# Weight sums of seven-product matrix multiplications: on the engines, or by copying and adding transfers in DRAM

## The chip, the core and the metric

The kernel runs on one core of a Trainium2 chip. The metric is the device time of one execution in microseconds; three runs of the kernel before gave 787.34, 787.57 and 787.62 us, a median of 787.57. The engines are named as in the profile: PE multiplies matrices, PEld loads its weights, DVE, ACT and POOL work on tiles, SP only issues transfers. Transfers are issued from the queue of SP, ACT or POOL, and all of them run on the same 16 DMA engines.

## What is computed

One decoder block on 512 positions of width 1024, in float32:

```python
h = rmsnorm(x, norm1_g);  z = h @ w_in + b_in          # (512, 1024) @ (1024, 6656)
u = glu(z);  u = conv31(u);  u = silu(layernorm(u));  y_a = u @ conv_w_out + conv_b_out
xb = conv4(z_rx);  hb = rg_lru(xb);  y_b = (hb * gelu(z_rg)) @ lru_w_out
m = sigmoid(z_ga) * y_a + sigmoid(z_gb) * y_b;  x = x + m @ w_mix_out
h = rmsnorm(x, norm2_g)
x = x + (silu(h @ ffn_w1) * (h @ ffn_w3)) @ ffn_w2      # (512,1024)@(1024,2816), twice; (512,2816)@(2816,1024)
out = rmsnorm(x, norm_f_g)
```

## The kernel before

**Precision.** Every float32 matrix is split into a high part (a rounded copy, made on ACT) and a low part (what the rounding took away, made by a subtraction on DVE or POOL, line 119). A product is the sum of three: high by high, high by low, low by high. A weight chunk is 128 x 1024 numbers (512 KB): SP loads it into one of four `raw` buffers, ACT casts it into one of five `hl` slots (line 123), DVE or POOL makes the low part, PE uses it. `weights(key, ahead)` makes chunks ready up to four chunks ahead of the one in use.

**Stages.** First projection (`z`, 52 tiles of 24 products, about 23 to 310 us), with the depthwise convolution on DVE and the gates of the recurrence (the `h` entries, `g` in the profile) running beside it in the order that the string `ORDER` writes out; then `yb` (the recurrence's output product), `ya` (the convolution's), the mixing product (`mxr`), the SwiGLU products (`f` for the first pair of tiles, `fr` for the others) and the last product (`or`).

**Seven products for eight.** The mixing product, ten of the eleven pairs of SwiGLU tiles (`SEVEN`, k = 1 to 10) and the last product go by a scheme of seven half-size products in place of eight (Strassen's, in Winograd's form). For it, weights are taken in quarters b11, b12, b21, b22, and four sums of quarters are needed: t1 = b12 - b11, t3 = b22 - b12, t2 = t3 + b11, t4 = b21 - t2. The activations get sums of their own (`pair`, `f_inputs`). For the mixing product the sums are made on DVE (`make_sums`, line 321), before and after.

**The sums for SwiGLU and the last product, before.** They are made in pieces of 128 x 1024 numbers: load four quarters to a `wsum` buffer (`piece_load`, line 396), four operations in place (`piece_sums`, lines 119 and 407), store four sums to DRAM (`piece_store`, line 413). There are 40 pieces for SwiGLU and 22 for the last product. In the first projection, `yb` and `ya` a generator (`make_f_sums`) takes one step per entry of `ORDER`, per tile of `yb` and per tile of `ya`: its loads are on SP's queue, its sums on POOL, its stores first on SP's, later on POOL's queue. From the SwiGLU stage on `out_step` starts the pieces of the last product after the plan `OUT_PIECES`: load and store on POOL's queue, sums on DVE. `tc.issue_after(...)` places an instruction behind another one on its engine. In the z stage PE, ACT, DVE and SP follow the written order; POOL is ordered by the planner, behind those marks.

**Pairing.** A pair k of SwiGLU tiles is the neighbours 2k and 2k + 1, and so are the two tiles of the last product's k. Two neighbours lie side by side in DRAM, so chunks of 256 columns are loaded (`f_chunks`: rows of 1 KB for the quarters, and 4 KB without a break for the stored sums); only b11, and all chunks of k = 1, 2, 3 but t2 and t1, are loaded by `f_both` in rows of 128 columns.

Of the kernel before, what the change touches and what calls it, by code (L numbers as in the profile page):

```python
# [35 lines left out]
SUMS_BEHIND = 3  # L36
# [11 lines left out]
PIECES = 4  # L48


OUT_PIECES = {0: "1", 1: "111", 2: "01", 3: "11", 4: "111", 5: "101", 6: "111", 7: "111", 8: "101", 9: "101", 10: "100"}
# [4 lines left out]
SUMS_AT, SUMS_STEP, SUMS_LAG, STORE_LAG = 3, 3, 2, 2  # L56
STORED_LAG = 3
SUMS_DENSE, SUMS_OWN, SUMS_EACH = 22, 40, (56, 68)


F_LATE, F_AT, OUT_MIX, MIX_LATE_LAG, LATE_LAG = 2, 6, 1, 2, 8
OUT_IN = 0
# [23 lines left out]
def tile_block(ctx, tc, a, out):  # L86
# [5 lines left out]
    wsums = pool("wsums", PIECES)  # L92
# [20 lines left out]


# [150 lines left out]
    class Quartered:  # L265
        def __init__(self, name, w, kh, lo, parts=(), step=None, on_pool=(), put_off=()):
# [3 lines left out]
            self.step = step or 1  # L270
            self.tile = lambda k, i: k + kh * i if self.step == 1 else 2 * k + i
# [3 lines left out]
            self.sums = {(n, k): self.all_sums[k][:, i, :] for i, n in enumerate(IN_PLACE) if n not in parts for k in range(kh)}  # L275
# [45 lines left out]
        def make_sums(self, k):  # L321
# [8 lines left out]
            if not self.parts:  # L330
                for i, v in enumerate(q):
                    nc.sync.dma_start(self.all_sums[k][:, 2 * i : 2 * i + 2, :], v.rearrange("p (m n) -> p m n", m=2))
                return
# [20 lines left out]
    WHERE = {  # L354
        "b21": ("b2", 0, True), "b22": ("b2", 1, False), "t2": ("t0", 0, True),
        "t1": ("t0", 1, False), "t3": ("t1", 1, True), "t4": ("t1", 0, False),
    }

    def f_both(n, k, lo=vec):

        def load(raw_t):
            for i, w_ in enumerate((w1, w3)):
                if n[0] == "b":
                    src = f_quarter(n, k, w_, 0, 4)
                else:
                    c, e, _ = WHERE[n]
                    src = f_sums[k][:, i, int(c[1]), :].rearrange("p (k n) -> p k n", k=4)[:, :, e * P : (e + 1) * P]
                newest["any"] = nc.sync.dma_start(raw_t[:, i * T : (i + 1) * T].rearrange("p (k n) -> p k n", k=4), src).ins

        wchunk(f"f{n}_{k}", load, 8, P, lo=lo)  # L370

    def f_chunks(k, some=("b2", "t0", "t1")):

        for n in some:
            for i, w_ in enumerate((w1, w3)):
                if n == "b2":
                    src = w_[:, 4:8, 2 * k * P : 2 * (k + 1) * P]
                else:
                    src = f_sums[k][:, i, int(n[1]), :].rearrange("p (k n) -> p k n", k=4)
                wchunk(f"f{n}{i}_{k}", src, 4, 2 * P, lo=vec)  # L380

    def f_piece(k, i, c):

        quarters = (w1, w3)[i].rearrange("p (h n) c -> p n h c", n=2)[:, c, :, 2 * k * P : 2 * (k + 1) * P]
        return f"{k}_{i}_{c}", [quarters], f_sums[k][:, i].rearrange("p m (k c n) -> p c m k n", k=2, c=2)[:, c]

    def o_piece(k, c):
        four = outq.w.rearrange("p (k h) (e n) -> p h k e n", h=2, e=2)
        cs = slice(256 * c, 256 * c + 256)
        return f"o{k}_{c}", [four[:, h, k, :, cs] for h in range(2)], outq.all_sums[k][:, :, cs]  # L390

    def piece_load(name, halves, queue=nc.sync):
        raw = wsums.tile([P, 1024], F32, tag="wsum", name=f"fws{name}")
        n = 1024 // len(halves)
        for h, src in enumerate(halves):
            queue.dma_start(raw[:, h * n : h * n + n].rearrange("p (e n) -> p e n", n=256), src)  # L396
        return raw

    def piece_sums(raw, dest, eng):
        if len(dest.shape) == 4:  # L400
            of = raw.rearrange("p (h k e n) -> p h e k n", h=2, k=2, e=2)
        else:
            of = raw.rearrange("p (h e n) -> p h e n", h=2, e=2)
        q11, q12, q21, q22 = (of[:, h, e] for h in range(2) for e in range(2))
        sub(eng, q22, q22, q12)
        sub(eng, q12, q12, q11)
        eng.tensor_tensor(out=q11, in0=q22, in1=q11, op=ALU.add)
        sub(eng, q21, q21, q11)

    def piece_store(raw, dest, queue=nc.sync):  # L410
        if len(dest.shape) == 4:
            dest = dest.rearrange("p m k n -> p (m k) n")
        return queue.dma_start(dest, raw.rearrange("p (m n) -> p m n", n=256))  # L413

    def make_f_sums():

        todo = f_todo[:-F_LATE] + [out_todo.pop(0) for _ in range(OUT_IN)]
        sums_due, stores_due = [], []
        n, next_at, stored = 0, SUMS_AT, [-9]
        while todo or sums_due or stores_due:
            if stores_due and (emitted[0] >= stores_due[0][0] or not (todo or sums_due)):
                stores_due.pop(0)[1]()
                stored[0] = n
            if sums_due and n >= sums_due[0][0]:
                sums_due.pop(0)[1]()
            if todo and n >= next_at and len(sums_due) + len(stores_due) + (n < stored[0] + STORED_LAG) < PIECES:  # L430
                next_at += SUMS_STEP - (n >= SUMS_DENSE) - (SUMS_EACH[0] <= n < SUMS_EACH[1])
                name, halves, dest = todo.pop(0)
                with tc.issue_after(newest["load"]):
                    raw = piece_load(name, halves)

                def sums(raw=raw, dest=dest, own=n >= SUMS_OWN):
                    with tc.issue_after(newest["sub"]):
                        piece_sums(raw, dest, pool_e)
                        if own:
                            piece_store(raw, dest, pool_e)  # L440
                            return

                    def stores():
# [1283 lines left out]
```

## Time and profile before

| | |
|---|---|
| median of three runs | 787.57 us (787.34 to 787.62) |
| profiled execution: span | 785.7 us |
| PE busy | 777.9 us, 99% |
| DVE busy | 682.8 us, 87% |
| ACT busy | 474.6 us, 60% |
| POOL busy | 362.3 us, 46% |
| SP's queue: packets, MB, share of 16 engines | 178066, 161.80, 68.4% |
| POOL's queue (software): packets, MB, share | 10272, 36.18, 13.2% |
| granted clock of PE | 0.998 |

The profiled execution took 785.7 us from its first to its last instruction; the runs' 787.57 us has about 1.9 us beside that span. A group of instructions reads: line, engine, operation, output <- inputs, how often, then busy time, mean of one, and the idle time of the engine just before with what ended it. A row of the chain of waits reads: start, length, what. A row of a stage has the busy time of PE, PEld, DVE, ACT and POOL with their counts of instructions, the granted clock, the mean busy share of the 16 DMA engines and GB/s. A row of a DMA queue has packets, MB and the share of 16 engines' time; a row of transfers has the issuing queue, how many, their size and, on POOL's queue, the median time to landing.

### The profile page before, as it was taken

The numbers are of one execution on the slowest core, as the hardware profiler recorded it, in microseconds if no ns is written. First come the engines' busy times: TensorE is split into PE (matmuls) and PEld (weight loads), VectorE is DVE, ScalarE is ACT, GpSimd is POOL, SyncE is SP. The second block draws the span as 40 slices with busy tenths as digits, with TensorE's granted clock in tenths as the row PEclk, the third lists the DMA queues.
The fourth block names the chain that finished last, engine by engine and source line by source line (L and its number), as shares of the span: only waits on it lengthen the run. The fifth ranks groups of instructions, "written<-read, shape, count | busy, mean of one in ns | idle before, by whom it ended". The sixth has DMA issues, their size and how long they took to land.

```text
span 785.7 us, 12502 instructions
## 1 busy us (share of the span) xinstructions
PE 777.9 (99%) x4327; PEld 680.0 (87%) x4327; DVE 682.8 (87%) x1074; ACT 474.6 (60%) x697; POOL 362.3 (46%) x353
## 2 busy tenths in 40 slices
PE   9999999999999999999999999999999999999996
PEld 8888888888888888888888898999999999888885
DVE  6389998889987988999799869899878888999956
ACT  8543678966785786574235675555554555556844
POOL 4367876789798988654440382122322321000000
PEclk9999999999999999999999999999999999999999
DMA  8556989899899966998978676699998998778652
GB/s 246 164 148 183 290 227 271 239 275 275 249 278 272 274 203 208 331 303 268 306 264 294 189 211 209 192 313 313 348 339 297 325 333 283 226 237 273 196 172 108
DMA packets 188561, 199.04 MB, mean 253 GB/s; under 512 B 15290, under 2 KB 149586, under 8 KB 188498
## 3 DMA queue, kind: packets, MB, share of 16 engines
q1 hardware_dynamic: 178066, 161.80, 68.4%
q0 software_dynamic: 10272, 36.18, 13.2%
q8 instruction: 34, 0.56, 0.3%
q14 instruction: 29, 0.24, 0.1%
q10 hardware_dynamic: 160, 0.27, 0.1%
HBM read 146.30 MB, written 38.80 MB: 236 GB/s over the span
## 4 chain that ended last, share of the span: by engine, by line
PE 98%; DMA 1%; DVE 0%; ACT 0%; SPq 0%; issue 0%
PE z L577 36%; PE fr L1440 25%; PE or L1204 13%; PE yb L577 7%; PE ya L577 6%; PE mxr L1204 5%; PE f L577 3%; PE g L1030 2%; PE fr L1495 1%; DMA x<-in_x_dram 1%; PE tx L638 0%; PE th L622 0%; PE z L695 0%; ACT of L1668 0%; PE orl L1204 0%; DVE n1j L659 0%
## 5 line engine op out<-in xcount | busy, mean ns | idle before, releaser
L830 DVE SCALAR_TENSOR_TENSOR cv<-u,par,cv 128x507 f32<-128x507 f32 (+15 forms) x240 | 162.2, 733 | 4.2 <-ACT cv L826 3.3
L119 POOL TENSOR_TENSOR hl_in<-raw_in,hl_in 128x1024 fp32r<-128x1024 f32 (+1 forms) x52 | 123.8, 2391 | 53.8 <-ACT hl_in L123 44.7
L119 POOL TENSOR_TENSOR fws<-fws 128x256 f32<-128x256 f32 x114 | 92.0, 810 | 44.1 <-DMA fws<-in_ffn_w_dram 38.8
L413 POOL DMA_DIRECT2D ot<-fwso x21 | 15.4, 733 | 132.9 <-DVE fwso L119 125.0
L1440 PE MATMUL fr<-hs_0h,hl_ft 128*128 128x256 f32 x320 | 59.2, 283 | 0.0
L123 ACT CAST hl_ft<-raw_ft 128x1024 fp32r<-128x1024 f32 x40 | 41.7, 1046 | 27.2 <-PE fr L1440 18.5
L119 DVE TENSOR_TENSOR hl_ft<-raw_ft,hl_ft 128x1024 fp32r<-128x1024 f32 x39 | 47.7, 1222 | 10.9 <-ACT hl_ft L123 10.8
L123 ACT CAST hl_in<-raw_in 128x1024 fp32r<-128x1024 f32 x50 | 51.4, 1047 | 1.7 <-PE z L577 1.1
L1440 PEld LDWEIGHTS fr<-hs_0h,hl_ft 128*128 128x128 f32 x320 | 50.6, 192 | 0.0
L1440 PE MATMUL fr<-hs_0l,hl_ft 128*128 128x256 f32 x160 | 45.3, 283 | 0.0
L119 DVE TENSOR_TENSOR hl_fb<-raw_fb,hl_fb 128x1024 fp32r<-128x1024 f32 x29 | 35.5, 1225 | 9.3 <-ACT hl_fb L123 9.3
L123 ACT CAST hl_fb<-raw_fb 128x1024 fp32r<-128x1024 f32 x30 | 31.5, 1049 | 17.9 <-PE fr L1440 8.8
L577 PE MATMUL z<-h10h,hl_in 128*128 128x512 f32 (+1 forms) x108 | 41.1, 382 | 0.0
L577 PE MATMUL z<-h12h,hl_in 128*128 128x512 f32 (+1 forms) x108 | 40.8, 379 | 0.0
L577 PE MATMUL z<-h13h,hl_in 128*128 128x512 f32 (+1 forms) x108 | 40.8, 379 | 0.0
L577 PE MATMUL z<-h14h,hl_in 128*128 128x512 f32 (+1 forms) x108 | 40.8, 379 | 0.0
L577 PE MATMUL z<-h15h,hl_in 128*128 128x512 f32 (+1 forms) x108 | 40.8, 379 | 0.0
L577 PE MATMUL z<-h16h,hl_in 128*128 128x512 f32 (+1 forms) x108 | 40.8, 379 | 0.0
L577 PE MATMUL z<-h11h,hl_in 128*128 128x512 f32 (+1 forms) x108 | 40.8, 379 | 0.0
L577 PE MATMUL z<-h17h,hl_in 128*128 128x512 f32 (+1 forms) x108 | 40.8, 379 | 0.0
L396 POOL DMA_DIRECT2D fwso<-in_ffn_w_dram x42 | 29.9, 716 | 23.7 <-DMA ot<-fwso 21.9
L119 POOL TENSOR_TENSOR hl_ot<-raw_ot,hl_ot 128x1024 fp32r<-128x1024 f32 x1 | 2.4, 2413 | 83.2 <-ACT hl_ot L123 83.2
(949 smaller groups left out, 2629.6 us busy)
## 6 DMA issues: line engine op xcount, KB each, us to landing
raw_in<-in_w_in_dram SPq DMA_DIRECT2D x51, 512.0 KB
fws<-in_ffn_w_dram SPq DMA_DIRECT2D x38, 512.0 KB
raw_ft<-fs SPq DMA_DIRECT2D x34, 512.0 KB
fs<-fws POOLq DMA_DIRECT2D x25, 512.0 KB, 5.2
fwso<-in_ffn_w_dram POOLq DMA_DIRECT2D x42, 256.0 KB, 7.1
ot<-fwso POOLq DMA_DIRECT2D x21, 512.0 KB, 6.0
raw_ob<-in_ffn_w_dram SPq DMA_DIRECT2D x33, 256.0 KB
raw_ot<-ot SPq DMA_DIRECT2D x33, 256.0 KB
```

The source lines that it names most:

```text
L119: return eng.tensor_tensor(out=o, in0=x, in1=y, op=ALU.subtract)
L123: copy(h, full)
L396: queue.dma_start(raw[:, h * n : h * n + n].rearrange("p (e n) -> p e n", n=256), src)
L413: return queue.dma_start(dest, raw.rearrange("p (m n) -> p m n", n=256))
L577: pe.matmul(ps, l, r, start=i == 0, stop=i == n - 1)
L830: vec.scalar_tensor_tensor(out=acc[:, s:], in0=u[c][:, : T - s], scalar=dw(c, s), in1=acc[:, s:], op0=ALU.mult, op1=ALU.add)
L1030: pe.matmul(ps[:HB], head_chunk[0][:ROWS_G, g, h % 2, m, :], ext[h][m][:ROWS_G], start=m == 0, stop=m == 1)
L1204: pe.matmul(banks[i][:, cs], l_[:, ts], r_[:, cs], start=start and n == 0, stop=stop and n == 2, skip_group_check=again)
L1440: pe.matmul(ps[:, HALVES[i]], lw[:, c, :], rx_, start=not (again or i or c or m), stop=bool(i and c == 3 and m == 2), skip_group_check=True,)
L1495: pe.matmul(self.r4[:, HALVES[i]], lw, rx_, start=not (i or c or m), stop=bool(i and c == 3 and m == 2), skip_group_check=True)
```

## The change

The sums for SwiGLU and the last product are made without any engine: transfers from DRAM to DRAM copy a quarter into the place of a sum, and adding transfers (with an accumulating operation) add another quarter to what lies there. They are issued from POOL's queue. Since a transfer can add but not subtract, the scheme is written with plus signs in the weights (t3 = b12 + b22, t2 = t3 + b11, t4 = t2 + b21, t1 = b11 + b12), and the minus signs go to the sums of activations and of results: `add` becomes `sub` and the other way round in `pair`, `f_inputs`, `rest`, `mix_end` and `out_end`. `make_sums` for the mixing product gets plus signs too and stays on DVE.

Tiles are paired eleven apart (k and k + 11), so that a transfer for SwiGLU covers ten tiles at once: 128 rows of 1280 numbers (5120 bytes), one for each of four chunks of rows, two weights and eight steps of the sums: 64 transfers of 655 KB. Those of the last product cover up to three k: 128 x 3 rows of 2 KB: 24 of 786 KB and 8 of 524 KB. Each sum is a list in which every transfer needs the one before: six long (t3, t2, t4) or two long (t1). Four lists take turns. One transfer is issued per step of the generator; there is a step per entry of `ORDER` (60, the first three empty), 12 in `yb`, 8 in `ya` and two for each k in the SwiGLU loop.

The SwiGLU chunks are now all loaded by `f_both`: two transfers of 256 KB, in rows of 128 columns (512 bytes). The low parts of `lo` and `co` chunks are made on POOL instead of DVE, and so are those of b22 and t3 for k from 4 on.

```diff
-            wchunk(f"lo{j}_{hf}", lru_out[:, 5 * hf : 5 * hf + 5, j * P : (j + 1) * P], 5, P, lo=vec)
+            wchunk(f"lo{j}_{hf}", lru_out[:, 5 * hf : 5 * hf + 5, j * P : (j + 1) * P], 5, P)
...
-        wchunk(f"co{j}", conv_out[:, :, j * P : (j + 1) * P], ND, P, lo=vec)
+        wchunk(f"co{j}", conv_out[:, :, j * P : (j + 1) * P], ND, P)
...
-            self.all_sums = [dram.tile([P, 4, T], F32, tag=f"{name}t_{k}", name=f"{name}t_{k}") for k in range(kh)]
+            self.all_sums = {n: dram.tile([P, kh, T], F32, tag=f"{name}{n}", name=f"{name}{n}") for n in IN_PLACE if n not in parts}
...
-            sub(vec, q22, q22, q12)
-            sub(vec, q12, q12, q11)
-            vec.tensor_tensor(out=q11, in0=q22, in1=q11, op=ALU.add)
-            sub(vec, q21, q21, q11)
+            add(q22, q22, q12)
+            add(q12, q12, q11)
+            add(q11, q22, q11)
+            add(q21, q21, q11)
...
-    f_sums = {k: dram.tile([P, 2, 2, 1024], F32, tag=f"fs{k}", name=f"fs{k}") for k in SEVEN}
+    f_sums = {(n, i): dram.tile([P, 4, KF * P], F32, tag=f"fs{n}{i}", name=f"fs{n}{i}") for n in IN_PLACE for i in range(2)}
+    f_cols = slice(min(SEVEN) * P, KF * P)
+
+    def dram_sums(quarter, sums):
+        b11, b12, b21, b22 = (quarter(i, h) for i in range(2) for h in range(2))
+        t1, t2, t3, t4 = (sums[n] for n in ("t1", "t2", "t3", "t4"))
+        copy = lambda o, x: pool_e.dma_start(o, x)
+        plus = lambda o, x: pool_e.dma_start(o, x, accum_op=ALU.add)
+        return [[(copy, t3, b12), (plus, t3, b22), (copy, t2, t3), (plus, t2, b11), (copy, t4, t2), (plus, t4, b21)], [(copy, t1, b11), (plus, t1, b12)]]
+
+    def f_jobs():
+        lists = []
+        for c in range(4):
+            for i, w_ in enumerate((w1, w3)):
+                quarter = lambda q, h: w_[:, 4 * q + c, h * KF * P + f_cols.start : h * KF * P + f_cols.stop]
+                lists += dram_sums(quarter, {n: f_sums[n, i][:, c, f_cols] for n in IN_PLACE})
+        return lists
+
+    def out_jobs():
+        lists = []
+        for k0 in range(0, KF, 3):
+            k1 = min(k0 + 3, KF)
+            quarter = lambda q, h: outq.w[:, q * KF + k0 : q * KF + k1, h * T : (h + 1) * T]
+            lists += dram_sums(quarter, {n: v[:, k0:k1, :] for n, v in outq.all_sums.items()})
+        return lists
+
+    def in_turn(lists, width):
+        lists = list(lists)
+        active = []
+        while lists or active:
+            while lists and len(active) < width:
+                active.append(lists.pop(0))
+            for l in list(active):
+                yield l.pop(0)
+                if not l:
+                    active.remove(l)
...
-        c, j = 4 * (int(n[1]) - 1), 2 * k + int(n[2]) - 1
+        c, j = 4 * (int(n[1]) - 1), k + KF * (int(n[2]) - 1)
...
-                    c, e, _ = WHERE[n]
-                    src = f_sums[k][:, i, int(c[1]), :].rearrange("p (k n) -> p k n", k=4)[:, :, e * P : (e + 1) * P]
+                    src = f_sums[n, i][:, :, k * P : (k + 1) * P]
...
-    def f_chunks(k, some=("b2", "t0", "t1")):
-    def f_piece(k, i, c):
-    def o_piece(k, c):
-    def piece_load(name, halves, queue=nc.sync):
-    def piece_sums(raw, dest, eng):
-    def piece_store(raw, dest, queue=nc.sync):
-    def make_f_sums():
...
+    def make_sums():
+        for _ in range(SUMS_AT):
+            yield
+        for jobs in (f_jobs(), out_jobs()):
+            for start, dst, src in in_turn(jobs, 4):
+                with tc.issue_after(newest["sub"]):
+                    start(dst, src)
+                yield
...
         elif k in SEVEN:
-            f_both("b11", k)
-            f_chunks(k)
+            for n in ("b11", "b21", "b22", "t2", "t1", "t3", "t4"):
+                f_both(n, k, pool_e if n in ("b22", "t3") else vec)
...
-        next(f_sums_steps, None)
+        for _ in range(1 + j % 2):
+            next(f_sums_steps, None)
...
             f_product(k, got, r3, "s4", "b22")
+            next(f_sums_steps, None)
             f_product(k, got, r1, "s2", "t2", True)
...
-            add(q, r5, q)
+            sub(vec, q, r5, q)
...
-            out_step(k)
             o7.release(KEPT.get(k, 0))
+            next(f_sums_steps, None)
             f_product(k, got, r7, "s3", "t3")
...
-            add(q, r7, q)
+            sub(vec, q, q, r7)
```

More of the change, by code (lines that the diff above doesn't have):

```diff
@@ L415, in make_f_sums @@
-    def make_f_sums():
[L421 to L443, printed above, removed]
-                        with tc.issue_after(newest["load"]):
-                            piece_store(raw, dest)
-                    stores_due.append((emitted[0] + STORE_LAG, stores))
-                if n >= SUMS_EACH[0]:
-                    sums()
-                else:
-                    sums_due.append((n + SUMS_LAG, sums))
-            n += 1
-            yield
@@ L1348, in mix_end @@
                 full(f_full[c][:, LO], c, LO)
-            for piece in made:
-                with tc.issue_after(newest["full"]):
-                    piece_sums(*piece, pool_e)
             for i in range(2):
-                plus(2 + i, 1, r7[i])
+                less(2 + i, 1, r7[i])
                 plus(2 + i, 0, r7[i])
@@ L1425, in f_product @@
     def f_product(k, got, ps, x_, w_, again=False, ahead=AHEAD, between=None):
-        both = w_ == "b11" or k in BEGUN + BEGUN_LATER and w_ not in ("t2", "t1")
-        n, e, first = WHERE.get(w_, (None,) * 3)
+        got[w_] = weights(f"f{w_}_{k}", ahead)
         for i in range(2):
-            if both:
-                if i == 0:
-                    got[w_] = weights(f"f{w_}_{k}", ahead)
-                h, l = (v[:, 4 * i : 4 * i + 4, :] for v in got[w_])
-            else:
-                if first:
-                    got[n, i] = weights(f"f{n}{i}_{k}", AHEAD - i)
-                h, l = (v[:, :, e * P : (e + 1) * P] for v in got[n, i])
+            h, l = (v[:, 4 * i : 4 * i + 4, :] for v in got[w_])
             for c, (xh, xl) in enumerate(f_in[x_]):
@@ L1445, in f_product @@
                 between()
-            if i == 0 and not both and not first:
-                emit_to(emitted[0] + 1)
-            due_sums()
     left = []
@@ L1588, in tile_block @@
             ffn_out(j, p1, p3)
-        out_step(k)
         if k + 1 in SEVEN:
@@ L1612, in loads @@
         elif k == 10:
-            assert not out_todo and out_at == [None, None]
             for h in range(2):
```

148 lines of the change are left out of this document (31 added, 117 removed).

## The prediction

> **What bounds the kernel now.** I read the page first (engines and chain), then the waits of PE, then the busy time by stage, then the transfers of three stages. From the page:
>
> ```profile
> PE 777.9 (99%) x4327; PEld 680.0 (87%) x4327; DVE 682.8 (87%) x1074; ACT 474.6 (60%) x697; POOL 362.3 (46%) x353
> ...
> PE 98%; DMA 1%; DVE 0%; ACT 0%; SPq 0%; issue 0%
> ```
>
> PE is busy for 777.9 of 785.7 us and the chain of waits that ended last is 98% PE. The waits of PE in the whole run, and two pieces of that chain:
>
> ```profile
> PE warm L546 <- DVE ones L538: 1.1, 1, 1.1
> PE tx L638 <- DVE x L678: 0.6, 1, 0.6
> ```
> ```profile
> 173.78 1.85 PE g L1030 x8
> 175.63 21.78 PE z L577 x96
> ```
>
> Both waits lie in the first microseconds. After them PE waits for nothing; 96 products of 512 columns take 21.78 us, 227 ns each, one tile of 24 in 5.45 us. The change keeps every product, so nothing that it takes off DVE, POOL or SP can shorten this chain: it can only leave PE alone, or stall it. What could stall it is read from the stages (columns: busy time of PE, PEld, DVE, ACT, POOL with counts, granted clock, mean busy share of the 16 DMA engines, GB/s):
>
> ```profile
> 23.00:310.00 287.00, 287.00 (x1288) 235.73 (x1287) 252.64 (x375) 199.44 (x267) 228.07 (x192) 1.00 0.84 237
> 310.00:366.00 56.00, 56.00 (x248) 46.30 (x247) 51.89 (x67) 33.95 (x52) 29.83 (x35) 1.00 0.93 302
> 366.00:410.00 44.00, 44.00 (x196) 36.44 (x195) 38.75 (x54) 14.04 (x18) 21.04 (x24) 1.00 0.89 289
> 410.00:450.00 40.00, 40.00 (x189) 33.36 (x188) 37.16 (x67) 23.51 (x41) 5.93 (x7) 1.00 0.76 246
> 500.00:675.00 175.00, 175.00 (x1459) 174.96 (x1458) 151.20 (x245) 90.15 (x126) 42.64 (x60) 1.00 0.93 310
> ```
> ```profile
> 120.00:140.00 20.00, 20.00 (x89) 16.21 (x88) 17.92 (x24) 17.79 (x23) 15.90 (x12) 1.00 1.04 277
> ```
>
> These are the first projection (z), the two output products (yb, ya), the mixing product (mxr) and the SwiGLU products (fr). The DMA engines are already 84 to 93% busy there; the highest stretch of 20 us is 1.04 with PE still gap free, so I take 1.04 as all that they can do.
>
> **Price of a packet.** Two rows give it: the loads of 512-byte rows between 20 and 40 us, and POOL's own queue in the SwiGLU stage (packets, MB, share of 16 engines):
>
> ```profile
> q1 hardware_dynamic: 5951, 3.24, 58.9%
> ```
> ```profile
> q0 software_dynamic: 6336, 22.02, 36.5%
> ```
>
> 58.9% of 16 x 20 us over 5951 packets is 31.7 ns for 544 bytes; 36.5% of 16 x 175 us over 6336 is 161 ns for 3475 bytes. A line through both is 7.6 ns + 0.0442 ns per byte: 30.3 ns for 512 B, 52.9 for 1 KB, 189 for 4 KB. So 512 KB cost all 16 engines 1.94 us in 512 B rows, 1.69 in 1 KB rows and 1.51 in 4 KB packets, 347 GB/s.
>
> **What goes.** The sums' transfers, by stage (z; yb and ya; SwiGLU; last column the landing time):
>
> ```profile
> fws<-in_ffn_w_dram SPq DMA_DIRECT2D x27, 512.0 KB
> fs<-fws SPq DMA_DIRECT2D x15, 512.0 KB
> fs<-fws POOLq DMA_DIRECT2D x11, 512.0 KB, 4.4
> ```
> ```profile
> fs<-fws POOLq DMA_DIRECT2D x12, 512.0 KB, 5.6
> fws<-in_ffn_w_dram SPq DMA_DIRECT2D x11, 512.0 KB
> ```
> ```profile
> raw_ft<-fs SPq DMA_DIRECT2D x30, 512.0 KB
> ot<-fwso POOLq DMA_DIRECT2D x20, 512.0 KB, 6.2
> ...
> raw_fb<-in_ffn_w_dram SPq DMA_DIRECT2D x14, 512.0 KB
> ```
>
> z: 42 x 1.69 + 11 x 1.51 = 88 us of DMA time. yb and ya: 11 x 1.69 + 12 x 1.51 = 37. SwiGLU: POOL's queue, 36.5% of 175 = 64. What stays is 0.84 x 287 - 88 = 153 us of 287; 0.93 x 56 + 0.89 x 44 - 37 = 54.5 of 100; 0.93 x 175 - 64 = 99 of 175. POOL and DVE lose the four sums of each piece; in z on POOL that is:
>
> ```profile
> L119 POOL TENSOR_TENSOR hl_in<-raw_in,hl_in 128x1024 fp32r<-128x1024 f32 x48 | 116.5, 2437 | 42.8 <-ACT hl_in L123 40.5 <-DMA raw_gate<-in_lru_wx_dram 0.9 <-DMA ext<-xb2l 0.8
> L119 POOL TENSOR_TENSOR fws<-fws 128x256 f32<-128x256 f32 x80 | 61.1, 767 | 5.7 <-DMA fws<-in_ffn_w_dram 2.2
> L407 POOL TENSOR_TENSOR fws<-fws 128x256 f32<-128x256 f32 x27 | 20.3, 756 | 1.8
> L413 POOL DMA_DIRECT2D fs<-fws x11 | 8.6, 785 | 2.1 <-POOL fws L119 1.8 <-PE z L577 0.3
> ```
>
> POOL is given back 61 + 20 + 9 = 90 us in z. Worth nothing on the path: PE waits for neither engine.
>
> **What comes.** 96 transfers from DRAM to DRAM on POOL's queue, one per step: 64 for SwiGLU (128 rows of 5120 B, 655 KB) and 32 for the last product (24 of 786 KB, 8 of 524 KB). Three steps are empty, so of the 60 entries of the first loop 57 carry one (z); the 12 steps of yb carry 7 and 5, ya 8 of the last product; 19 are left to the two slots per k of the SwiGLU loop (11 of 786 KB, 8 of 524 KB). At 347 GB/s the bytes once over take 57 x 1.89 = 108 us in z; 7 x 1.89 + 13 x 2.27 = 43 in yb and ya; 11 x 2.27 + 8 x 1.51 = 37 in SwiGLU. That is about what goes (88, 37, 64). The open price is what each byte counts for, since three of every eight transfers are copies and five add into what lies there; no row of before shows either kind. Copy: it reads once and writes once, as a packet of the q0 row does, so factor 1; at most 2, if having both ends in DRAM costs as a load and a store one after the other. Add: two reads and a write; at least 1 (the add rides along), at most 3 (each at the price of a transfer). I take 1 and 2: a packet that must fetch both operands holds its engine as two q0 packets would. Mean factor (3 x 1 + 5 x 2) / 8 = 1.625, between 1 and (3 x 2 + 5 x 3) / 8 = 2.6.
>
> The Trainium skill bears on this twice, both times against the change. "DMA: Bandwidth & Descriptors", Latency and other measured facts, gives copies between HBM tensors 214 GB/s as their full rate: 655 KB would be 3.06 us, a factor of 1.62 for all eight, which gives the sum below. "Collectives: The Full Stack", The bandwidth ceiling, says that a reducing transfer reaches half the rate of a copying one, since both operands are read on one ring (measured there 1.93); with both rules the factor would be 2.6, the upper bound. No run shows either yet.
>
> The SwiGLU loads get dearer too: the pairs are eleven tiles apart, so a chunk reads rows of 512 B where it had 4 KB (sums) and 1 KB: 30 x (1.94 - 1.51) + 14 x (1.94 - 1.69) = 16 us, and 99 becomes 115.
>
> **The sum.** Demand at factor 1.625, over 1.04, against the stage: z 153 + 175 = 328, / 1.04 = 316, 29 us too much. yb and ya 54.5 + 69.4 = 124, / 1.04 = 119, 19 too much, of which the mixing stage takes 0.24 x 40 = 9.6: 9.5 left. SwiGLU 115 + 60 = 176, / 1.04 = 169 of 175, nothing. Together 38.5 us on 785.7 us. The median of the runs, 787.57, lies 1.9 above this span; I add the same and get 826.
>
> How the excess reaches PE: an adding transfer waits on POOL for the one before it in its list, which was issued only four steps earlier (four lists take turns). Behind the waiting issue on POOL stand the low parts of the weights (hl_in, 2437 ns each), which the next z tile needs; five hl slots hold at most about four tiles ahead, 4 x 5.45 = 22 us of cover, and a lasting shortage uses that up. The weight loads on SP's queue share the same engines and come late as well.
>
> **Costed at nothing, with what hides it.** The low parts of lo and co move from DVE to POOL, as do b22 and t3 of k from 4 on; by the hl_in row a full one is 2.44 us on POOL, 16 x 1.5 + 8 x 2.44 = 43 us in yb and ya, where POOL is busy 51 of 100 and loses the sums. POOL's 57 issues in z, at 0.785 us (L413 row) to twice that, are 45 to 90 us of the 90 freed. Cover is the four tiles; if POOL is held up, these low parts are the work that comes late, at one product's 5.45 us per tile. Reversed signs swap add for subtract: same instructions.
>
> **Rivals.** (1) Not slower: an added byte costs like a loaded one, factor near 1. Then z needs 261 of 287, yb and ya 97 of 100, SwiGLU 152 of 175, and PE notices nothing: 787.6, 786.5 to 789. It decides below a factor of (1.04 x 287 - 153) / 108 = 1.35 in z and (104 + 9.6 - 54.5) / 43 = 1.38 in yb and ya. For it: the 1.04 stretch without a gap in PE; the larger rows. Against: the second operand must be read. (2) Both ends in DRAM make copies and adds dear, factor 2 to 2.6: at 2 the stages lack 68, 25 and 7 us, together 100, so 888; at 2.6 they lack 132, 51 and 30: 1000. (3) There is DMA time enough, but the chain is too tight: in runs of short steps (two heads are 1.85 us of PE in the chain's row) four steps pass in some 8 us, a landing takes 4.4 to 6.2 us for 512 KB, more for 655 KB with two reads, and POOL waits a few us each time with low parts behind it. The 22 us cover most; I price one tile's delay at two places, 2 x 5.45 = 11, at most: 790 to 798. (4) Faster: a relieved engine ends something sooner at the head or the tail, where PE is not the limit. The change touches neither; under 1 us.
>
> **How the numbers follow.** Chances: forecast (factor 1.35 to 2) 0.42; (1) 0.26; (2) 0.17; (3) 0.11; (4) 0.04. Slower by over 0.2% (1.6 us, what can be told apart here): 0.42 + 0.17 + 0.11 = 0.70. Within: 0.26. Faster: 0.04. The forecast alone spans 790 to 888. The range starts at 786, just under (1), and ends at 900, a factor of 2.07; above lies most of (2), about 0.15.
>
> **What would show it.** Right: q0 packets twice as dear per byte as 161 ns for 3475; DMA shares near 1.0 through z, yb and ya; PE waits on POOL's hl_in, hl_lo and hl_co, and POOL in front of them on its own DRAM transfers; SwiGLU nearly gap free. Wrong: PE still at 778 us without waits and shares under 0.95 (rival 1); SwiGLU stalled as well (2); PE gaps at moderate shares (3).

## The result and the profile after

The changed kernel takes 839.45 us (median of four runs, 832.78 to 843.09) against 787.60: a ratio of 1.065, interval 1.0603 to 1.0697. It is slower, 52 us; the forecast was 826 with a range of 786 to 900. The profiled execution is the fastest of the four: a span of 831.0 us, 45.3 more than before. What the other runs have beyond it is in no profile. All ratios are of fast runs alone; one run of e8 and two of the four of e12 were more than 1.5% slower than the fastest of their kernel, and since the profiled run of each is one of these, neither stands in the table of stages.

The page of the changed kernel, engines, chain of waits and queues:

```profile
PE 795.0 (96%) x4327; PEld 688.8 (83%) x4327; DVE 627.7 (76%) x944; ACT 472.8 (57%) x697; POOL 320.3 (39%) x241
...
PE 55%; DMA 24%; DVE 7%; ACT 4%; POOL 3%; SPq 3%; issue 3%; DVEq 0%; ACTq 0%; POOLq 0%
```

PE was 98% of the chain and is 55%; transfers have 24%. DVE and POOL lost 55 and 42 us of work, which bought nothing. The stages of the changed kernel (columns as in the prediction; z, yb, ya, mixing product, first SwiGLU tiles, the rest of SwiGLU):

```profile
23.00:336.00 313.00, 296.09 (x1296) 240.22 (x1295) 242.84 (x373) 201.25 (x270) 182.19 (x135) 0.97 0.96 250
336.00:391.00 55.00, 55.00 (x244) 45.33 (x243) 38.74 (x50) 31.98 (x49) 27.95 (x22) 1.00 0.93 254
391.00:441.00 50.00, 46.52 (x192) 37.48 (x192) 35.01 (x41) 12.25 (x17) 25.93 (x17) 0.93 1.00 275
441.00:490.00 49.00, 43.99 (x186) 34.88 (x185) 42.08 (x74) 25.14 (x43) 7.02 (x7) 0.93 0.85 273
490.00:544.00 54.00, 50.57 (x326) 46.60 (x325) 35.03 (x64) 27.94 (x47) 18.80 (x19) 0.97 0.75 197
544.00:720.00 176.00, 176.00 (x1469) 176.00 (x1468) 126.19 (x155) 92.92 (x132) 46.52 (x28) 1.00 0.89 238
```

Length of each stage, from its first product to the next stage's first product in the trace, in us; the stages are those of the profiled execution, and the labels are those of the experiments below:

| kernel | z | yb | ya | mixing | SwiGLU | median of runs |
|---|---|---|---|---|---|---|
| before | 302.8 | 54.9 | 43.5 | 39.9 | 225.1 | 787.6 |
| changed | 327.1 | 54.9 | 50.2 | 49.0 | 230.1 | 839.45 |
| e1, adds as copies | 304.6 | 54.9 | 45.5 | 46.4 | 225.1 | 795.57 |
| e2, no transfers | 302.7 | 54.9 | 43.5 | 39.9 | 225.1 | 788.11 |
| e3, SwiGLU's only | 327.6 | 54.9 | 43.5 | 39.9 | 225.1 | 813.38 |
| e4, last product's only | 302.7 | 54.9 | 44.3 | 49.3 | 231.5 | 802.58 |
| e5, shorter rows | 331.5 | 56.2 | 56.2 | 46.4 | 231.3 | 838.64 |
| e6, low parts on DVE | 326.8 | 88.7 | 43.5 | 39.9 | 230.3 | 851.22 |
| e7, later steps | 331.2 | 54.9 | 53.3 | 46.0 | 242.0 | 849.14 |
| e9, e4 with shorter rows | 302.8 | 54.9 | 46.3 | 49.5 | 228.4 | 804.04 |
| e10, e3 spread | 315.7 | 54.9 | 43.7 | 42.6 | 225.1 | 808.21 |
| e11, all spread | 319.8 | 54.9 | 43.5 | 48.5 | 268.4 | 855.53 |

Of the 45.3 us, 24.3 are in z, 6.7 in ya, 9.1 in the mixing product and 5.0 in SwiGLU, all of that in its first tiles; the last product is unchanged.

What PE, ACT and POOL waited for in the changed kernel (total us, times, longest), first PE, then ACT, then POOL:

```profile
PE g L976 <- DMA ext<-xb4h: 9.3, 1, 9.3
PE z L523 <- ACT hl_in L120: 3.5, 2, 1.9
PE fr L1383 <- ACT si L1296: 3.4, 1, 3.4
PE z L523 <- POOL hl_in L116: 3.4, 2, 1.7
```
```profile
ACT hl_fb L120 <- DMA raw_fb<-in_ffn_w_dram: 39.5, 10, 13.6
ACT hl_in L120 <- DMA raw_in<-in_w_in_dram: 39.0, 11, 12.1
ACT hl_co L120 <- DMA raw_co<-in_conv_w_out_dram: 23.8, 6, 12.7
ACT hl_ft L120 <- DMA raw_ft<-fst: 16.7, 14, 4.0
```
```profile
POOL fst L346 <- DMA fst<-in_ffn_w_dram: 8.9, 2, 5.6
POOL ot L347 <- DMA ot<-ot: 8.4, 1, 8.4
...
POOL fst L347 <- DMA fst<-fst: 4.5, 1, 4.5
```

What is late comes from SP's queue: weight loads, and once the gathering of rows for a head (`ext`). POOL waited for its own transfers 22 us in the whole run, and no long wait of PE follows from that. The largest single stall of PE lasts from 127.7 to 137.0 us, and the stretch from 118 us on shows how the loads get late. The two queues' packets, MB and share of the engines there, in the changed kernel, and the one queue in the same stretch before:

```profile
q0 software_dynamic: 576, 2.62, 64.0%
q1 hardware_dynamic: 2599, 1.87, 37.7%
```
```profile
q1 hardware_dynamic: 6814, 5.12, 101.0%
```

POOL's transfers hold 64% of the engines, and SP's queue moves 1.87 MB; at its average over z (40.82 MB in 313 us) it would move 2.5 MB in these 19 us. The 5.12 MB of before hold the sums' own loads and stores too, so they are no measure of what is missing. In the timeline of SP and then of PE, the issue of one gathering transfer takes 10.32 us (the median of its kind is 0.53), and PE waits at the head's product. That SP was held because its queue took no more is the likely reading, but no run shows it:

```profile
120.02 10.32 SPq L938 DMA_DIRECT2D ext<-xb4h  x1
```
```profile
137.02 2.08 PE L976 MATMUL g<-ext,hl_gate 120*80 120x512 f32 x4 [9.33 <-DMA ext<-xb4h]
```

### The profile page after: what moved, and what is told of

Read it like the earlier page. It is cut to its first block, busy times and chain, and to the rows that moved or that the text cites. A ratio compares the mean times of both kernels' runs of the same rounds, so it can differ in the third digit from the quotient of the medians.

```text
span 831.0 us, 12241 instructions
## 1 busy us (share of the span) xinstructions
PE 795.0 (96%) x4327; PEld 688.8 (83%) x4327; DVE 627.7 (76%) x944; ACT 472.8 (57%) x697; POOL 320.3 (39%) x241
## 3 DMA queue, kind: packets, MB, share of 16 engines
q1 hardware_dynamic: 187410, 132.96, 54.9%
q0 software_dynamic: 17792, 65.02, 32.1%
HBM read 178.80 MB, written 71.30 MB: 301 GB/s over the span
## 4 chain that ended last, share of the span: by engine, by line
PE 55%; DMA 24%; DVE 7%; ACT 4%; POOL 3%; SPq 3%; issue 3%; DVEq 0%; ACTq 0%; POOLq 0%
PE fr L1331 23%; PE z L523 14%; PE or L1148 13%; DMA raw_in<-in_w_in_dram 7%; DMA th<-tg 2%; PE mxr L1148 2%; DMA mxws<-in_w_mix_out_dram 2%; DMA raw_fb<-in_ffn_w_dram 2%; DMA x<-in_x_dram 2%; DMA ext<-xb6h 2%; DMA raw_co<-in_conv_w_out_dram 2%; DMA mxt<-mxws 2%; POOL hl_in L116 2%; DMA raw_lo<-in_lru_w_out_dram 2%; DVE cv L776 1%
## 5 line engine op out<-in xcount | busy, mean ns | idle before, releaser
L116 POOL TENSOR_TENSOR hl_fb<-raw_fb,hl_fb 128x1024 fp32r<-128x1024 f32 x8 | 19.3, 2414 | 139.4 <-ACT hl_fb L120 139.4
L116 DVE TENSOR_TENSOR hl_ft<-raw_ft,hl_ft 128x1024 fp32r<-128x1024 f32 x32 | 44.4, 1387 | 11.2 <-ACT hl_ft L120 11.2
L523 PE MATMUL z<-h10h,hl_in 128*128 128x512 f32 (+1 forms) x108 | 42.8, 398 | 7.6 <-ACT hl_in L120 3.5
L1331 PE MATMUL fr<-hs_0l,hl_ft 128*128 128x256 f32 x160 | 45.3, 283 | 0.0
L116 DVE TENSOR_TENSOR hl_fb<-raw_fb,hl_fb 128x1024 fp32r<-128x1024 f32 x22 | 26.8, 1220 | 20.6 <-ACT hl_fb L120 20.6
L116 POOL TENSOR_TENSOR hl_ft<-raw_ft,hl_ft 128x1024 fp32r<-128x1024 f32 x8 | 19.5, 2434 | 48.5 <-DVE ov L1347 30.2
L1347 DVE TENSOR_TENSOR ou<-c 128x256 f32<-128x256 f32 x20 | 20.3, 1019 | 22.8 <-ACT c L1346 22.8
```

What stands on the lines that cost most here:

```text
L116: return eng.tensor_tensor(out=o, in0=x, in1=y, op=ALU.subtract)
L523: pe.matmul(ps, l, r, start=i == 0, stop=i == n - 1)
L1331: pe.matmul(ps[:, HALVES[i]], lw[:, c, :], rx_, start=not (again or i or c or m), stop=bool(i and c == 3 and m == 2), skip_group_check=True,)
L1347: newest["now"] = vec.tensor_tensor(out=dst, in0=c[:, LO], in1=c[:, HI], op=ALU.mult).ins
```

## The experiments

The theories: A, engine time: an add holds its DMA engine for two packets, and the stages run out of engine time. B, turns: a weight load's small packet gets a turn for each of POOL's large packets, so loads are late whenever POOL's transfers run. C, the rest of the change (512-byte rows, low parts on POOL) is the cost. And the prediction's rival 3, the chain of waits on POOL is too tight.

### e1: adds as copies

```diff
-        plus = lambda o, x: pool_e.dma_start(o, x, accum_op=ALU.add)
+        plus = copy
```

> The five adding transfers of every eight become plain copies of the same bytes at the same places; the sums are not formed, so the values are not the reference's. Theory A (engine time: an add holds its engines for two packets, and the stages run out of engine time): z needs about 153 us for the rest plus 57 transfers at some 1.6 to 1.9 us, 244 to 261 of 287 us, so no stall: 787 to 791 us, PE idle only at the ends; the price of a packet in POOL's queue falls from about 325 ns per 5120 bytes to about 200. Theory B (turns: a 512-byte packet of SP's weight loads gets one turn for every packet of POOL's queue, so loads come late whenever POOL's transfers are under way, whatever the total): packets of some 200 ns still stand between, stalls shrink to about half: 800 to 815 us. Theory C (512-byte rows and low parts on POOL are the cost): no change, about 839 us.

795.57 us (794.26 to 797.66), ratio 1.0099, interval 1.0082 to 1.0117. 44 of the 52 us go with the adds. Some 8 remain at the median where theory A expected 0 to 3; the profiled run, the slowest of the four, has 10: 1.8 in z, 2.0 in ya, 6.5 in the mixing product. POOL's queue in this run, whole span of 795.9 us:

```profile
q0 software_dynamic: 14976, 65.02, 22.8%
```

22.8% of 16 x 795.9 us for 65.02 MB is 229 ns per 5120 bytes. The changed kernel moves the same bytes with 32.1% of 831.0 us, 336 ns:

```profile
q0 software_dynamic: 17792, 65.02, 32.1%
```

Adds are four of every eight transfers, and not five as the prediction and the expectation of e1 count them: each of t3, t2, t4 and t1 is begun by a copy and ended by an add. The transfers for SwiGLU in the changed kernel, adds (line 347) and then copies (line 346):

```profile
L347 POOL DMA_DIRECT2D fst<-in_ffn_w_dram x32: 791/828/1467, 70.6 to 377.4; - x32
L346 POOL DMA_DIRECT2D fst<-in_ffn_w_dram x16: 517/540/754, 43.0 to 348.5; - x16
L346 POOL DMA_DIRECT2D fst<-fst x16: 517/562/789, 81.1 to 368.4; - x16
```

So an add costs (336 - 1/2 x 229) / (1/2) = 443 ns, 1.93 times a copy on the average. The single packets of 5120 bytes in the trace of the changed kernel, ns at some quantiles:

```
quantile            5%   10%   25%   50%   75%   90%
5120 B, copies+adds 196   196   196   402   402   404
5120 B, e1 (copies) 196   196   196   196   196   233
```

Undisturbed, a copy is 196 ns and an add 402, 2.05 times as long. Why is not shown: the profile's page counts 178.80 MB read from HBM and 71.30 MB written in the changed kernel and in e1 alike, so a second read by the adds does not appear there.

### e2: no transfers

```diff
-                    src = f_sums[n, i][:, :, k * P : (k + 1) * P]
+                    src = f_quarter({"t1": "b12", "t2": "b11", "t3": "b22", "t4": "b21"}[n], k, w_, 0, 4)
...
-        for jobs in (f_jobs(), out_jobs()):
-            for start, dst, src in in_turn(jobs, 4):
-                with tc.issue_after(newest["sub"]):
-                    start(dst, src)
-                yield
```

The last product's loads of sums are pointed at quarters in the same way.

> No transfers in DRAM at all: the loads of t1 to t4 for SwiGLU and the last product read quarters of the weights in place of sums (same sizes and row lengths), so the values are not the reference's. Everything else of the change stays: pairs eleven apart, 512-byte rows, low parts on POOL, signs. Theories A and B: 787.6 us within 0.2%, and PE without waits after the first microseconds. Theory C: most of the 52 us remain, 820 to 840 us.

788.11 us, ratio 1.0004, interval 0.9995 to 1.0014: no difference that can be measured. PE's waits are those of the head again:

```profile
PE warm L489 <- DVE ones L481: 1.1, 1, 1.1
PE tx L581 <- DVE x L621: 0.4, 1, 0.4
```

Theory C falls. Pairing, 512-byte rows, low parts on POOL and the signs cost nothing by themselves; the 52 us come with the DRAM transfers.

### e3 and e4: one half of the transfers each

```diff
-        for jobs in (f_jobs(), out_jobs()):
+        for jobs in (f_jobs(),):
```

and for e4, with SwiGLU's loads pointed at quarters,

```diff
-        for jobs in (f_jobs(), out_jobs()):
+        for _ in range(64):
+            yield
+        for jobs in (out_jobs(),):
```

> Only the 64 transfers for SwiGLU; the last product's t loads read quarters of the weights, so its part of the values is not the reference's. Theories A and B: the z stage stays 24 us too long, ya, mixing product and first SwiGLU tiles are back to before (43.5, 39.9, 49.6 us): 810 to 815 us. If the later stages stay late without transfers of their own, the delay is carried over from z: 825 us or more.

> Only the 32 transfers for the last product, at the steps they have in the changed kernel (5 in yb, 8 in ya, 19 in SwiGLU); SwiGLU's t loads read quarters of the weights, so the values are not the reference's. Theory A: z back to 302.8 us from first tile to yb; yb and ya alone have room for 13 transfers (54.5 us of the rest and about 44 for 13 transfers at 3.4 us, of 100), so at most a few us: 788 to 795 us. Theory B: ya, mixing product and first SwiGLU tiles stay 15 to 21 us too long, since each stall there is one load taking turns with POOL's packets: 803 to 809 us.

e3: 813.38 us, ratio 1.034 (1.0306 to 1.0374), 24.8 us of it in z. e4: 802.58, ratio 1.0183 (1.0166 to 1.02), in the mixing product (9.4) and SwiGLU's first tiles (6.4). So the two stalls are separate; 25.7 and 14.9 us make 41 of the 52, and the rest comes with both together (ya loses 6.7 in the changed kernel and under 1 in either half). e4 was outside theory A's 788 to 795 and a little under theory B's 803 to 809: by theory A's sum the transfers fit, yet PE stalls. The timeline of POOL in e4, from where PE is at SwiGLU's first tiles, and the two queues between 482 and 499 us, in which a `raw_fb` load took 16.9 us:

```profile
476.01 1.25 POOL L347 DMA_DIRECT2D ot<-in_ffn_w_dram  x1
...
478.90 1.73 POOL L347 DMA_DIRECT2D ot<-in_ffn_w_dram  x1
...
482.95 2.12 POOL L347 DMA_DIRECT2D ot<-in_ffn_w_dram  x1
...
483.73 2.45 POOL L346 DMA_DIRECT2D ot<-ot  x2
```
```profile
q0 software_dynamic: 1246, 3.44, 83.0%
q1 hardware_dynamic: 2361, 1.18, 26.2%
```

Five transfers of 786 KB are issued between 476 and 486 us, and in the stretch from 482 to 499 us the weight loads have a quarter of the engines. The code has one transfer per step, but a step is only a place in POOL's queue: POOL issues it as soon as it gets there, whatever PE is doing. What paces POOL is its own low parts, and there are few of them at that point.

### e5 and e9: shorter rows, the same bytes

```diff
-                quarter = lambda q, h: w_[:, 4 * q + c, h * KF * P + f_cols.start : h * KF * P + f_cols.stop]
-                lists += dram_sums(quarter, {n: f_sums[n, i][:, c, f_cols] for n in IN_PLACE})
+                quarter = lambda q, h: w_[:, 4 * q : 4 * q + 4, h * KF * P + cols.start : h * KF * P + cols.stop]
+                lists += dram_sums(quarter, {n: f_sums[n, i][:, :, cols] for n in IN_PLACE})
```

where `cols` is the c-th quarter of the columns (320). e9 does the like in e4: half the columns of the last product's rows for up to six k at a time.

> The 64 transfers for SwiGLU cover the same sums in rows of 1280 bytes in place of 5120: each takes a quarter of the columns for all four chunks of rows, instead of all columns for one chunk. Values as the reference's. Theory A (engine time): bytes and adds are the same, packets a little dearer each per byte, so the z stage stays 24 us too long or gains a few: 835 to 850 us. Theory B (turns): a load's 512-byte packet waits for an add of about 105 ns in place of 402, so loads land sooner and POOL's transfers later; z loses most of its excess, 815 to 825 us, and POOL waits more on its own transfers than 22 us.

> As the run with the last product's 32 transfers alone (SwiGLU's t loads read quarters of the weights, values not the reference's), with rows of 1 KB in place of 2 KB: each transfer covers half the columns for twice as many k. That run took 802.6 us, 15 us more than before. Theory A (engine time): the adds cost about a tenth more engine time, 802 to 806 us. Theory B (turns): a load waits for packets half as long, its landing falls from about 13 to 8 us, and about half the 15 us go: 793 to 798 us.

e5: 838.64 us, ratio 1.0658 (1.0628 to 1.0689); e9: 804.04, ratio 1.0208 (1.0191 to 1.0225). Neither gains anything, and theory B's figures are missed. In a stall of e5, 120 to 140 us, POOL's queue still has most of the engines, with packets of 1280 bytes for its adds (its copies still went as packets of 5120 bytes):

```profile
q0 software_dynamic: 1805, 3.01, 70.7%
q1 hardware_dynamic: 3071, 2.14, 42.5%
```

So a packet of a third of the time did not give the loads a larger part to speak of, and theory B, in the form that the size of POOL's packets decides, falls as the main cause. A smaller effect is not excluded, since the shorter rows made the adds dearer: 120 ns for 1280 bytes, four of which replace one of 402 ns. POOL's queue has 33.9% of 841.5 us in e5, 285 us, in place of 267, and in e9 108 in place of e4's 98; a gain of that size would not be seen. What sets the shares of the two queues stays open.

### e6: the low parts of lo and co back on DVE

```diff
-            wchunk(f"lo{j}_{hf}", lru_out[:, 5 * hf : 5 * hf + 5, j * P : (j + 1) * P], 5, P)
+            wchunk(f"lo{j}_{hf}", lru_out[:, 5 * hf : 5 * hf + 5, j * P : (j + 1) * P], 5, P, lo=vec)
...
-        wchunk(f"co{j}", conv_out[:, :, j * P : (j + 1) * P], ND, P)
+        wchunk(f"co{j}", conv_out[:, :, j * P : (j + 1) * P], ND, P, lo=vec)
```

> One part of the change undone: the low parts of the lo and co chunks are made on DVE again, as before. Values as the reference's. Theories A and B: nothing, 833 to 843 us, since the low parts wait for loads and not for POOL. If POOL's queue is what holds ya (transfers in front of low parts): ya back from 50 to 44 us, 826 to 835 us.

851.22 us, ratio 1.0809 (1.0793 to 1.0825): 12 us slower than the changed kernel, which no theory had expected. yb takes 88.7 us in place of 54.9, while ya and the mixing product are back to before. PE's longest wait, and the transfers of the last product in the timeline of POOL (count, durations, first and last start), in e6 and then in the changed kernel:

```profile
PE yb L523 <- ACT hl_lo L120: 20.2, 4, 8.6
```
```profile
L346 POOL DMA_DIRECT2D ot<-in_ffn_w_dram x8: 716/780/1052, 349.8 to 670.1; - x8
```
```profile
L346 POOL DMA_DIRECT2D ot<-in_ffn_w_dram x8: 716/764/1199, 383.4 to 649.7; - x8
```

Without low parts between them POOL issues the transfers of yb and ya as fast as each finds the one before it landed (56 us of such waits in place of 22): the first for the last product goes out 34 us earlier though PE is no further, and all 13 are out by 398 us, before ya starts at 424. In the changed kernel they go out from 383 to 445 us. The low parts that were moved to POOL are what had spread them.

### e7: thirteen steps later

```diff
+            if not later:
+                later.append(1)
+                for _ in range(13):
+                    yield
...
             next(f_sums_steps, None)
+            next(f_sums_steps, None)
```

The first addition stands behind SwiGLU's transfers in the generator, the second at both slots of the SwiGLU loop.

> The 13 transfers for the last product that were issued in yb and ya come later: none there, and four per k in place of two in the SwiGLU loop. Values as the reference's. Theories A and B: ya and the mixing product are back to before (43.5 and 39.9 us, 16 us won), and the SwiGLU loop has 32 transfers (about 99 us of engine time) beside 115 us of loads in 176 us, so it runs over by 20 to 40 us: 840 to 865 us. If SwiGLU has room: 820 to 828 us.

849.14 us, ratio 1.0778 (1.0762 to 1.0794). The time lies where A put it, but not by A's way: ya and the mixing product did not recover (53.3 and 46.0 us), since the transfers did not come later.

```profile
L347 POOL DMA_DIRECT2D ot<-in_ffn_w_dram x16: 1131/1232/2107, 411.0 to 637.5; - x16
L346 POOL DMA_DIRECT2D ot<-in_ffn_w_dram x8: 716/770/1167, 387.4 to 602.8; - x8
```

The first starts at 387.4 us against 383.4 with z 4 us longer: POOL ran ahead through the empty steps. With four per k they were all issued by 638 us (709 in the changed kernel), and SwiGLU took 242 us. So this run did not test what it was made for; it shows the missing pace once more.

### e8: eight lists in turn

```diff
-            for start, dst, src in in_turn(jobs, 4):
+            for start, dst, src in in_turn(jobs, 8):
```

> Eight lists take turns in place of four, so that every transfer comes eight steps after the one it needs. Values as the reference's. Theory A (engine time): nothing changes, 833 to 843 us. The prediction's rival 3 (the chain is too tight, POOL waits for its own transfers with low parts behind): those waits, 22 us in the changed kernel, go, and 5 to 12 us with them: 822 to 832 us.

838.83 us, ratio 1.064 (1.0613 to 1.0668), the changed kernel's own. The edit did what it was for: POOL waits 8 us for its own transfers in the profile, in place of 22, and nothing is gained. Rival 3 falls.

### e10 and e11: spread

```diff
-            for start, dst, src in in_turn(jobs, 4):
+            for n, (start, dst, src) in enumerate(in_turn(jobs, 4)):
+                if n % 6 == 5 and not spread:
+                    yield
```

e10 has this with SwiGLU's transfers alone. e11 has all, four per k in the SwiGLU loop, and

```diff
             for n in ("b22", "t2", "t1", "t3"):
-                f_both(n, k)
+                f_both(n, k, pool_e if n in ("b22", "t3") else vec)
```

> As the run with SwiGLU's 64 transfers alone (813.4 us; the last product's t loads read quarters of the weights, values not the reference's), with every seventh step left empty, so that 49 in place of 57 fall into the z stage and 15 in place of 7 into yb and ya. Theory A (engine time): z needs 153 us and 49 x 2.6 = 127, 280 of 287; yb and ya 54.5 and 39, 94 of 100; both fit, with little to spare: 788 to 800 us. If the stalls come from bursts of transfers and not from the sum over the stage: 805 to 813 us.

> All sums, spread: SwiGLU's transfers with every seventh step empty as above; the last product's 3 in ya and four per k in the SwiGLU loop, with the low parts of b22 and t3 on POOL for all ten k, so that POOL can't run ahead there. Values as the reference's. Theory A (engine time): z, ya and the mixing product nearly as before, SwiGLU needs 115 us for loads and some 90 for 29 transfers, 205 of 176, so 20 to 30 us over: 808 to 822 us. If pace alone is the cause: 788 to 800 us.

e10: 808.21 us (804.23 to 809.09), ratio 1.0252 (1.0226 to 1.0279): 5 us better than e3 at the median, in the band expected of bursts. In its profile z is 12.9 us too long, at a mean share of 0.93, and a single wait is most of that:

```profile
PE g L983 <- DMA ext<-xb4h: 10.7, 1, 10.7
```
```profile
23.00:313.00 290.00, 279.23 (x1246) 228.42 (x1244) 238.95 (x371) 195.72 (x262) 170.04 (x122) 0.98 0.93 246
```

So fewer transfers in a stage help, and a single load can still come late when the stage as a whole has engine time left. e11: 855.53 us, ratio 1.0865 (1.0845 to 1.0886), worse than the changed kernel and above both bands: ya is as before and z wins 7 us, but the mixing product still loses 8.6 us and SwiGLU, into which the transfers are now held back, runs 43 us over where 20 to 30 were expected. What is taken out of one stage comes back in another.

### e12: two copies for an add

```diff
+        def plus(o, x):
+            made[0] += 1
+            s_ = scratch[len(o.shape), made[0] % 8]
+            pool_e.dma_start(s_[:, : o.shape[1]], x)
+            return copy(o, x)
```

> Each add is replaced by two plain copies of the same bytes, one to its place and one to a spare place in DRAM; the sums are not formed, values not the reference's. Theory A (an add costs what holding the engines for two packets costs, and nothing else matters): as the changed kernel, 830 to 848 us, against 795.6 with one copy per add. If an add has a cost of its own in waiting or in POOL's descriptors: under 820 us.

Ratio 1.0768, interval 1.0717 to 1.0819, that is some 848 us: at the upper end of A's band, some 52 us above one copy per add (e1) and 9 above the add itself. Each add became two copies, and the time went up by one per cent: an add costs the kernel about what two copies cost. A cost of its own of a few us could not be told apart here.

No version beat the kernel before: PE waits for nothing there, and e2 shows that the changed kernel without its transfers only equals it.

## Why the prediction was right, and where it was not

**PE's chain can only be left alone or stalled.** Right: the products are the same 4327, and e2 is within 0.2% of before.

**Copy 1, add 2, mean factor 1.625.** The two prices are right, the count is wrong. Copies cost 229 ns per 5120 bytes against 234 by the line, a factor of 0.98, and adds 443, a factor of 1.89. But adds are four of eight transfers and not five (e1), so prices of 1 and 2 make a mean of 1.5. With it the prediction's own sum gives 16 us in z and 4 after it, a forecast of 808 us in place of 826: the miscount brought the forecast nearer to the result, by luck. Measured, the mean is 336 / 234 = 1.44, and rival 2, which needs 2 to 2.6, falls. Of the two rules named there, that a reducing transfer has half the rate of a copying one (the Trainium skill, "Collectives: The Full Stack", The bandwidth ceiling) agrees with 402 against 196 ns; the reason that it gives, two reads, is not shown here. The 214 GB/s that the Trainium skill gives for copies between HBM tensors ("DMA: Bandwidth & Descriptors", Latency and other measured facts; measured there on the queues of SP and ACT) are no limit here: 5120 bytes in 196 ns are 418 GB/s over 16 engines, and 229 ns are 358.

**What stays in each stage.** Right: SP's queue takes 48.3% of 313 us in z, 151 (predicted 153), and 65.8% of 176 us in SwiGLU, 116 (predicted 115).

```profile
q1 hardware_dynamic: 65657, 40.82, 48.3%
q0 software_dynamic: 8160, 37.20, 47.3%
```
```profile
q1 hardware_dynamic: 61166, 32.67, 65.8%
```

**What the engines can do in a stage: 1.04.** The figure holds, but the stretch that it was set against is the step that failed, and two other errors hid it. In z POOL's queue took 47.3% of 313, 148 us (175 predicted, of which 13 are the miscount). 151 and 148 over 1.04 are 288 us: by the prediction's own formula, with the measured price, z would have lost about 1 us. It lost 24.3. The changed kernel's stages up to 300 us show where:

```profile
23.00:43.00 20.00, 20.00 (x113) 17.40 (x112) 8.68 (x13) 12.00 (x17) 9.53 (x5) 1.00 0.47 128
43.00:70.00 27.00, 27.00 (x121) 22.36 (x120) 25.64 (x53) 10.59 (x19) 16.33 (x14) 1.00 0.83 240
70.00:300.00 230.00, 213.09 (x907) 170.67 (x906) 181.25 (x269) 148.32 (x197) 134.76 (x103) 0.96 1.03 267
```

All of PE's idle time in z, 16.9 us, lies after 70 us, and there the engines give 1.03. The first transfer for the sums goes out at 43.0 us and the first add at 70.6, so the engine time left over before that is of no use to them, though the sum counts it as room. From 70 us to the end of z the two queues have

```profile
q0 software_dynamic: 7584, 34.57, 52.6%
q1 hardware_dynamic: 54653, 34.47, 48.1%
```

of 266 us: 140 and 128, together 268, which over 1.04 is 258 us. Before, PE needed 241 us from there to the end of z (70 to 311). That is 17 us too much, against 16.9 us of idle PE; the other 7.4 us are products at a lower clock (last section), which the prediction left out. So the 29 us forecast for z came near by errors that offset each other: too many adds on one side, too much room and no loss of clock on the other. The count from 70 us on was made after the fact, and it does not cover every run: e10 has 244 us by it, over 1.04 235 of 241, and still waits 10.7 us for one gathering.

**Yb and ya lose 19, of which the mixing stage takes 9.6.** Wrong in place and size: yb lost nothing, ya 6.7, the mixing product 9.1, SwiGLU's first tiles 5.0; 21 in place of 9.5. The step that failed is that a transfer goes out with its step of PE's order. POOL's queue is not paced by PE's steps but by its own work and waits (e4, e6, e7), so the transfers come in bursts: in the changed kernel five of the last product's are issued between 429 and 436 us, just before the mixing product starts at 441. It then stalls at a mean share of 0.85, and SwiGLU's first tiles at 0.75, with engine time to spare.

**SwiGLU, nothing.** Right for its steady part, 175.68 us in both chains.

**How the excess reaches PE.** The way named first, low parts stuck on POOL behind a waiting transfer, did not happen to any extent: 22 us of such waits, and eight lists in place of four change nothing. The way named second did: loads on SP's queue come late. The largest chance was put on the right mechanism, engine time taken by adds (e1: 44 of 52 us); in the mixing product and SwiGLU's first tiles it acts by bursts and not by the sum of a stage.

**Costed at nothing: the low parts of lo and co on POOL.** Right as a price, but e6 shows that they have a worth: without their pace the kernel is 12 us slower.

## What to carry to other kernels

An adding transfer in DRAM cost the DMA engines about two copies (443 against 229 ns per 5120 bytes). Here these engines were 84 to 93% busy before, and work moved to them from engines that PE did not wait for was paid in late loads. Judge such a move by the stretch in which the new transfers can really run, and by bursts, not only by the mean of a stage: while POOL's transfers were under way, the loads on the other queue had a quarter to two fifths of the engines (26% in e4, 38% in the changed kernel, 42% in e5). A step in the program paces a transfer only if something in its own queue waits for the work that it is to keep pace with (e6, e7).

## What the runs showed of the hardware that was not expected

**A stall costs PE more than its length.** The stages of the changed kernel around the wait for the head's rows (columns as above, granted clock third from the end):

```profile
127.00:131.00 4.00, 0.68 (x4) 0.22 (x2) 3.21 (x6) 0.00 (x0) 0.00 (x0) 0.89 1.01 270
131.00:135.00 4.00, 0.00 (x0) 0.00 (x0) 0.00 (x0) 1.11 (x2) 0.00 (x0) 0.50 1.12 315
135.00:139.00 4.00, 1.98 (x5) 1.24 (x6) 2.25 (x4) 3.92 (x5) 3.35 (x3) 0.50 0.68 152
139.00:141.00 2.00, 2.00 (x8) 1.58 (x7) 2.00 (x3) 1.99 (x4) 0.00 (x0) 0.66 0.82 308
141.00:143.00 2.00, 2.00 (x10) 1.65 (x9) 0.99 (x2) 0.72 (x1) 1.20 (x1) 1.00 1.11 350
```

The wait ends at 137.0 us, but the clock is still 0.50 and comes back to 1.00 only after 139 us. Over z PE idled 313 - 296.1 = 16.9 us and the stage grew by 24.3: the other 7.4 are products at a lower clock, 0.97 on the mean of the stage. The Trainium skill has the rule ("TensorE: Matmul & The Clock Gate", Part 1: after an idle window of some 3.4 us the array runs at half rate until it has been busy as long again), and the trace agrees with it at this stall: 9.3 us without a product, and 1.00 again 2 to 4 us after the restart. The rule does not cover all: from 96 to 98 us the clock was 0.50 after two gaps of 1.9 and 1.7 us with two products between them, each gap shorter than that window. The prediction had left the clock out of its sum.

**An issue can take as long as a stall.** One issue on SP took 10.32 us, with the engines at 1.05 from 120 to 130 us, and every load that stands behind it on SP went out later. The median of its kind is 0.53 us. What held it is not shown; a queue that takes no more would do it.
